# A decoder trunk that streams its weights: a weight ring by last use, and other places for the seven-product pairs of the up panels

## The chip, the core and the metric

The kernel runs on one core of one Trainium2 chip. The metric is the time of one execution on the device in microseconds (us), the median of several runs. The engines of the core that matter here: PE (TensorE, matrix multiplications), DVE (VectorE, operations of two tensors), ACT (ScalarE, scaled copies and functions), POOL (GpSimd, which here issues transfers) and SP (SyncE, whose queue issues the transfers of weights). Each engine works through its own list of instructions in order, and waits for the others by semaphores.

## What is computed

Two decoder layers on 256 tokens of 2048 channels, in float32. A layer adds the output of a mixer (gated linear attention in layer 0, forgetting attention in layer 1, each with heads that attend to 256 memory tokens) and then that of a channel mixer, which has most of the work:

```python
def conv_ffn(h, w_up, conv_w, conv_b, w_down):
    u = causal_dwconv(h @ w_up, conv_w, conv_b)
    a, val = split_cols(u, [FFN_HIDDEN, FFN_HIDDEN])
    return (jax.nn.silu(a) * val) @ w_down
...
    for i in range(DEPTH):
...
        h = rmsnorm(x, norm_ffn[i])
        x = x + conv_ffn(h, ffn_w_up[i], ffn_conv_w[i], ffn_conv_b[i], ffn_w_down[i])
    return rmsnorm(x, norm_final)
```

`FFN_HIDDEN` is 5632, so `w_up` has 2048 x 11264 numbers and `w_down` 5632 x 2048, and all weights together are read once from the chip's memory in an execution.

## The kernel before

**Units.** The weights lie in memory as a list of units of 128 x 1024 float32 numbers (512 KB). For each unit `split_unit` issues one transfer on SP into a raw slot (L232), ACT rounds it to the matmul's type (`whi`, L242), and DVE takes the rest, `wlo` = raw - `whi` (L243). There are five buffers of each. PE multiplies activations that are split in the same way, in three terms (high by high, low by high, high by low), so a single unit is twelve matmuls into four accumulators (L421), eight that read `whi` and four that read `wlo`.

**The ring of raw slots.** `raw_slot` hands out raw slots by a running index, modulo the length of the list `slots`. The list has five slots of its own tile, `home`, in the whole program. In the channel mixer two `guest` slots (tile `raw2`) are appended at the start and cut off at the end; since the modulus changes from 5 to 7 and back, the next index after such a change can fall on any slot. The guest tile comes from a pool in which the mixer's last blocks (`blk`) lie before it: they are transposed by DVE (L1637) and stored by SP to memory (`far<-blk`, L659), to be read back in another layout (L664).

**Panels and pairs.** The up projection goes in 11 panels of 16 units, the down projections in panels between groups of them (after the up panels 0 to 4, 5 to 7 and 8 to 10). In some places two neighbouring units are done as a "pair with sevens", in `pair_steps`: a scheme of seven products p1 to p7 in place of eight, 21 matmuls instead of 24. It needs four casts on ACT (L391, named w1 to w4 here by their order), four subtractions for their low parts on DVE (L392) and four subtractions of raw blocks on DVE (L446 to L449), one built on the other; w3 is cast from the second's result, w4 from the last's. A panel with one pair has it in place 6 of the 16 (counted from 0). The up panels in `MORE_IN` have two pairs, of the units 6 and 7 and 11 and 12, in places 4 and 9. The pairs' token sums are ready from the start of the channel mixer or of the first panel.

**After a panel's last pair** `early` puts together the results of its products: L1513 and L1514 on ACT, then on DVE L1515, which adds p6, and L1516 to L1518, then L1520 on ACT. At the panel's end `late` scales and adds the four accumulators (L1524) and transposes them (L1475); POOL stores the result and loads it back in runs of tokens.

**Taps.** Of each panel so turned, ACT makes the three taps of the convolution (L1425, 12 of 128 x 256 each for a half panel), DVE adds them (L1432, twice), ACT takes the silu (L1438), DVE multiplies by the gate (L1445) and splits the product (L537 on ACT, L538 on DVE) for the down projection; some products also get token sums (L485 to L488, L696, L697). `tick`, called after each unit and twice after a pair, hands out these steps by a credit per unit, so they stand between the units' casts and subtractions.

**Order.** The program is written in this order; `high_priority` moves loads, casts and subtractions of the units ahead of PE's use, and `issue_after` keeps a step behind a named instruction. The order of each engine's list is fixed when the kernel is built.

Of the kernel before, what the change touches and what calls it, by code (L numbers as in the profile page):

```python
# [37 lines left out]
MORE_IN = (1, 2, 5, 6, 7, 8, 9, 10)  # L38
SCRATCH = 4096
RAWS = 5  # L40


LEVELS = (64, 16, 4)
# [2 lines left out]
NUNIT = 1024  # L46
# [102 lines left out]
def _trunk(ctx: ExitStack, tc: tile.TileContext, xt, xtok, memt, wp, wgu, gns, gfin, cnv, par, msk, out):  # L149
    nc = tc.nc  # L150
    where, _ = _layout()
# [34 lines left out]

    loads, casts, lows, ends, last_mm, sent = [], [], [], [], [], []
    home = rear.tile([P, RAWS * NUNIT], F32, name="raw")
    slots, taken = [home[:, i * NUNIT : (i + 1) * NUNIT] for i in range(RAWS)], [0]

    def raw_slot():

        taken[0] += 1
        return slots[taken[0] % len(slots)]
    scratch = [sm]
    parked = []

# [194 lines left out]
            lows.append(V.tensor_tensor(lo[:, :n], src, hi[:, :n].bitcast(F32), ALU.subtract))  # L392
        return hi, lo

    def pair_steps(units, src, sums, flip, pool, early, late, ahead=0):

        bank = {}
        fast, slow = ("p1", "p5", "p7", "p6"), ("p2", "p3", "p4", "x")
        accs, works = (slow, fast) if flip else (fast, slow)
        tags = {n: ("acc", 4) for n in accs}  # L400
        tags.update(zip(works, (("o", 1), ("s", 2), ("s", 2), ("t", 1))))
        begun = set()
        sums = dict(sums)
        n = len(units)
        single = [k for k in range(n) if k not in sums and k - 1 not in sums]
        plan = []
        at = 0
        while at < n:
            if at + ahead in sums:
                plan.append(at + ahead)  # L410
                at += 2
            else:
                plan.append(single.pop(0))
                at += 1
        end = [k for k in plan if k in sums]

        def mm(name, x, w, last):
            if name not in bank:
                tag, bufs = tags[name]
                bank[name] = (pacc.tile([P, 512], F32, name="acc", tag="acc") if tag == "acc" else work(tag, bufs))  # L420
            r = TE.matmul(bank[name], x, w, start=name not in begun, stop=last)  # L421
            begun.add(name)
            return r

        def tok(k, b):
            return [src[k][:, part, b * P : (b + 1) * P] for part in range(2)]

        def three(name, x, w, last=False):
            for i, (a, b) in enumerate(((0, 0), (1, 0), (0, 1))):
                r = mm(name, x[a], w[b], last and i == 2)  # L430
            return r

        places = (("p2", 0, 0), ("p4", 1, 0), ("p3", 0, 1), ("x", 1, 1))
        for k in plan:
            if k in sums:
                with tc.high_priority(offset=AHEAD):
                    ra, rb = raw_slot(), raw_slot()
                    with tc.issue_after(loads[-1].ins):
                        for t, (off, _, w) in ((ra, units[k]), (rb, units[k + 1])):
                            loads.append(nc.sync.dma_start(t, wp[off : off + P * w].rearrange("(p n) -> p n", p=P)))  # L440
                st = [[sums[k][:, part, j, :] for part in range(2)] for j in (3, 0, 1, 2)]
                done = k == end[-1]
                w1 = split_more(ra[:, :512], 512)
                w2 = split_more(rb, 1024)
                with tc.high_priority(offset=AHEAD):
                    V.tensor_tensor(ra[:, :512], ra[:, 512:], ra[:, :512], ALU.subtract)  # L446
                    V.tensor_tensor(ra[:, 512:], rb[:, 512:], ra[:, 512:], ALU.subtract)  # L447
                    V.tensor_tensor(rb[:, 512:], rb[:, 512:], ra[:, :512], ALU.subtract)
                    summed = V.tensor_tensor(rb[:, :512], rb[:, :512], rb[:, 512:], ALU.subtract)  # L449
                three("p1", tok(k, 0), [t[:, :512] for t in w1], done)  # L450
                three("p2", tok(k + 1, 0), [t[:, :512] for t in w2])
                three("p3", st[3], [t[:, 512:] for t in w2])
                with tc.issue_after(summed.ins):
                    w3 = split_more(ra, 1024)
                three("p5", st[0], [t[:, :512] for t in w3], done)
                three("p7", st[2], [t[:, 512:] for t in w3], done)
                w4 = split_more(rb, 1024)
                three("p6", st[1], [t[:, 512:] for t in w4], done)
                last_mm.append(three("p4", tok(k + 1, 1), [t[:, :512] for t in w4]))
                if done:  # L460
                    with tc.issue_after(casts[-1].ins), tc.issue_after(lows[-1].ins):
                        early(bank)
                yield -1
                yield -1
                continue
            else:
                w = split_unit(units[k])
                last = k == n - 1
                steps = [(low, *place) for low in range(2) for place in places]
                if last:  # L470
                    steps.sort(key=lambda t: places.index(t[1:]))
                for low, name, b, h in steps:
                    for part in range(2 - low):
                        r = mm(name, tok(k, b)[part], w[low][:, h * 512 : (h + 1) * 512], last and low == 1)
                    if last and low:
                        ends.append(r)
                        late(b, h, bank[name])
                last_mm.append(r)
            yield k
# [875 lines left out]
    def down_pair(l, p, f, src, sums, flip, pool, temps, then=None):  # L1355

        def early(bank):
            t0, t1 = temps()
            S.activation(t0, bank["p1"], AF.Copy)
            add_to(f)(0, t0)  # L1360
            V.tensor_tensor(t0, bank["p6"], t0, ALU.add)
            V.tensor_tensor(t1, bank["p7"], t0, ALU.add)
            add_to(f)(1, t1)
            add_to(f + 1)(1, t1)
            add_to(f + 1)(1, bank["p5"])
            V.tensor_tensor(t0, bank["p5"], t0, ALU.add)
            add_to(f + 1)(0, t0)

        def late(b, h, a):
            held_back = then is not None and h and not b and then.rooms is not None  # L1370
            with tc.issue_after(then.turned[-1].ins) if held_back else nullcontext():
                add_to(f + h)(b, a)
            if then is not None:
                then(f + h, b)

        return pair_steps(where["down", l, p, f], src, sums, flip, pool, early, late)

    def add_out(key, src, then=None, spare=None, last=None, first=0, hooks=None, late=1):

# [23 lines left out]
    def ffn(l, nx, h, m, ys, zs, landing, then, pool, temps, last=None, spare=None):  # L1403
        with tc.tile_pool(name=f"ffn{l}", bufs=1) as fp:
# [3 lines left out]
            up_sums = {k: held("usum", k) for k in (*SEVEN_UP, SEVEN_MORE)}  # L1408
            rooms = {i: held("dsum", i) for i in range(2)}
            guest = pool.tile([P, 2 * NUNIT], F32, name="raw2")  # L1410
            slots.extend(guest[:, i * NUNIT : (i + 1) * NUNIT] for i in range(2))
            cw = fp.tile([P, 4 * 88], F32, name="cw")
            nc.sync.dma_start(cw, cnv[l])
            taps = [fp.tile([P, 2, 2, T + i], F32, name=f"tap{i}") for i in range(3)]
# [2 lines left out]
            count = [0, 0, 0]  # L1417
            sums = {}
# [85 lines left out]
            def up_pair(j):  # L1504

                count[2] += 1
                second = j // 4 in MORE_IN
                turns = [turn(j + 2 * h_, 7 if not h_ and j // 4 + 1 in MORE_IN else 8) for h_ in range(2)]
                u = {}

                def early(bank):
                    u.update({(b, h_): temps(2 * b + h_) for b in range(2) for h_ in range(2)})
                    S.activation(u[0, 1], bank["p1"], AF.Copy)  # L1513
                    S.activation(u[0, 0], bank["p1"], AF.Copy, scale=scale(0))  # L1514
                    V.tensor_tensor(u[0, 1], bank["p6"], u[0, 1], ALU.add)  # L1515
                    V.tensor_tensor(u[1, 0], bank["p7"], u[0, 1], ALU.add)  # L1516
                    V.tensor_tensor(u[0, 1], bank["p5"], u[0, 1], ALU.add)
                    V.tensor_tensor(u[1, 1], bank["p5"], u[1, 0], ALU.add)  # L1518
                    for b, h_ in ((0, 1), (1, 0), (1, 1)):
                        S.activation(u[b, h_], u[b, h_], AF.Copy, scale=scale(b))  # L1520

                def late(b, h_, a):
                    with tc.issue_after(turned_last[0].ins) if h_ and not b else nullcontext():
                        V.scalar_tensor_tensor(u[b, h_], a, scale(b), u[b, h_], ALU.mult, ALU.add)  # L1524
                    turns[h_](b, u[b, h_])

                return pair_steps(where["up", l, j], h, {k: up_sums[k] for k in (*SEVEN_UP, SEVEN_MORE)[: 1 + second]},
                                  count[2] % 2, pool, early, late, 2 * second)

            def first(k):  # L1530
                {2: lambda: nx.land(landing[0]), 3: nx.take, 8: nx.col,
# [64 lines left out]
            else:  # L1596
                hooks = {(2, 3): then.land, (2, 5): then.land, (2, 7): then.take, (3, 1): then.take, (3, 2): then.land,
                         (3, 5): then.take}
                for f, step, at in ((2, f2, 3), (3, f3, 0)):
                    for u in range(at, 8):  # L1600
                        step(u)
                        hooks.get((f, u), int)()
            del slots[RAWS:]

    def preparing(name, dst, pool, far, kept=None, tag="blk", queue=nc.sync):

# [204 lines left out]
```

## Time and profile before

| what | value |
|---|---|
| median of three runs | 2221.41 us (2220.82 to 2221.58) |
| profiled execution | 2219.84 us |
| its span in the profile | 2218.0 us |
| mean granted clock of TensorE | 0.997 |
| HBM read, written | 469.62 MB, 43.79 MB |
| transfers of units on SP (`raw<-wp`, 512 KB) | 741, 4.6 us from issue to landing |

In a row of a timeline stand the start (us from the span's start), the time until the end of the last of the instructions grouped in it, engine, line, operation, output and inputs by the program's names, shapes, and the count; in brackets how long the engine was idle ahead of it, and what released it. `SPq` is SP's queue of transfers. Matmuls overlap by a part of their length, so their rate is read from start to start. PE's clock (PEclk) is 1 at full rate.

### The profile page before, as it was taken

The page shows a single profiled execution, that of the slowest core. Times are in us where ns is not written, and L with a number is a line of the kernel's source. Part 1 is how long each engine was busy: PE and PEld are TensorE (multiplying, and loading weights), DVE is VectorE, ACT ScalarE, POOL GpSimd, SP SyncE. Part 2 cuts the span into 40 slices and gives each one's busy share as a digit, 9 for nine tenths or more (in the row PEclk, how much of TensorE's full clock was granted, in tenths as well). Part 3 has the DMA queues.
Part 4 walks back from the last instruction along what each step waited for, and adds up shares of the span by engine and source line. Part 5 has one row for each costly group of instructions (what it writes and reads, how often), then busy time and mean ns, then how long its engine had stood idle before and what let it go on. Part 6 is the DMA issues. An engine that isn't in the chain of part 4 may idle for free.

```text
span 2218.0 us, 30190 instructions
## 1 busy us (share of the span) xinstructions
PE 2196.9 (99%) x10285; PEld 1846.7 (83%) x10285; DVE 1828.6 (82%) x2715; ACT 1437.8 (65%) x2280; POOL 136.8 (6%) x257
## 2 busy tenths in 40 slices
PE   9999999999999999999999999999999999999998
PEld 7888888878888888888888998877888888888886
DVE  7768976679988889889987569668998888988996
ACT  6655655557887568647865555445788657765874
POOL 0000000001100000001010000000100000100000
PEclk9999999999999999999999999999999999999999
DMA  9766666776777667666877667666687667776683
GB/s 360 260 222 217 199 207 230 252 231 223 258 250 239 199 228 256 231 207 224 268 246 245 219 207 235 224 217 223 224 263 248 222 203 245 242 236 211 230 283 113
DMA packets 166291, 515.41 MB, mean 232 GB/s; under 512 B 20780, under 2 KB 42552, under 8 KB 166136
## 3 DMA queue, kind: packets, MB, share of 16 engines
q1 hardware_dynamic: 149064, 460.99, 63.2%
q0 software_dynamic: 16496, 51.71, 7.4%
q8 instruction: 80, 1.31, 0.2%
q10 hardware_dynamic: 576, 0.79, 0.1%
q14 instruction: 75, 0.61, 0.1%
HBM read 469.62 MB, written 43.79 MB: 231 GB/s over the span
## 4 chain that ended last, share of the span: by engine, by line
PE 96%; DVE 2%; ACT 1%; DMA 1%; issue 0%; SPq 0%; DVEq 0%; ACTq 0%
PE acc L421 29%; PE acc L347 26%; PE ps_s L421 15%; PE ps_o L421 7%; PE ps_t L421 7%; PE acc L273 3%; PE acc L318 3%; PE ps_s L347 2%; PE acc L377 2%; PE acc L271 1%; PE ps_s L1044 0%; DMA raw<-wp 0%; ACT whi L242 0%; PE ps_o L710 0%; PE ps_s L710 0%
## 5 line engine op out<-in xcount | busy, mean ns | idle before, releaser
L243 DVE TENSOR_TENSOR wlo<-raw,whi 128x1024 fp32r<-128x1024 f32 (+2 forms) x685 | 812.5, 1200 | 222.9 <-ACT whi L242 200.8
L242 ACT ACTIVATE whi<-raw 128x1024 fp32r<-128x1024 f32 (+2 forms) x685 | 704.3, 1045 | 347.8 <-PE acc L347 131.2
L347 PE MATMUL acc<-whi,B 128*128 128x512 f32 (+3 forms) x1248 | 290.9, 369 | 0.0
L391 ACT ACTIVATE whi<-raw 128x1024 fp32r<-128x1024 f32 (+1 forms) x184 | 173.7, 953 | 179.4 <-DVE raw L447 65.7
L347 PEld LDWEIGHTS acc<-whi,B 128*128 128x128 f32 x1248 | 226.8, 188 | 28.1
L392 DVE TENSOR_TENSOR wlo<-raw,whi 128x1024 fp32r<-128x1024 f32 (+1 forms) x184 | 198.3, 1084 | 26.8 <-ACT whi L391 23.8
L421 PE MATMUL acc<-whi,mix 128*128 128x512 f32 x746 | 191.7, 392 | 8.7 <-ACT whi L242 8.7
L421 PE MATMUL acc<-whi,B 128*128 128x512 f32 x720 | 186.9, 389 | 0.0
L421 PEld LDWEIGHTS acc<-whi,mix 128*128 128x128 f32 x746 | 141.2, 189 | 38.7 <-ACT whi L242 9.2
L347 PE MATMUL acc<-wlo,B 128*128 128x512 f32 (+3 forms) x624 | 159.1, 369 | 0.0
L421 PEld LDWEIGHTS acc<-whi,B 128*128 128x128 f32 x720 | 135.1, 188 | 28.5 <-ACT whi L242 0.5
L347 PEld LDWEIGHTS acc<-wlo,B 128*128 128x128 f32 x624 | 114.2, 188 | 14.6
L1425 ACT ACTIVATE tap<-yzu,cw 128x256 f32<-128x256 f32 x264 | 120.7, 534 | 5.4 <-DMA yzu<-far 5.4
L1425 ACT ACTIVATE tap<-fvt,cw 128x256 f32<-128x256 f32 x264 | 120.2, 530 | 3.1 <-DMA fvt<-far 3.1
L1432 DVE TENSOR_TENSOR tap<-tap,tap 128x1024 f32<-128x1024 f32 x88 | 106.7, 1213 | 9.0 <-ACT tap L1425 9.0
L421 PE MATMUL acc<-wlo,mix 128*128 128x512 f32 x373 | 105.0, 392 | 0.0
L421 PE MATMUL acc<-wlo,B 128*128 128x512 f32 x360 | 103.8, 389 | 0.0
L421 PE MATMUL ps_s<-whi,mix 128*128 128x512 f32 x374 | 103.8, 389 | 0.0
L421 PE MATMUL ps_s<-whi,B 128*128 128x512 f32 x324 | 89.9, 389 | 0.0
L421 PEld LDWEIGHTS acc<-wlo,mix 128*128 128x128 f32 x373 | 70.6, 189 | 14.8
L421 PEld LDWEIGHTS ps_s<-whi,mix 128*128 128x128 f32 x374 | 70.2, 188 | 14.6
L421 PEld LDWEIGHTS acc<-wlo,B 128*128 128x128 f32 x360 | 67.6, 188 | 14.0
(503 smaller groups left out, 3912.8 us busy)
## 6 DMA issues: line engine op xcount, KB each, us to landing
raw<-wp SPq DMA_DIRECT2D x741, 512.0 KB, 4.6
fvt<-far POOLq DMA_DIRECT2D x100, 128.0 KB, 5.2
raw<-wp SPq DMA_DIRECT2D x32, 384.0 KB, 3.4
far<-yu POOLq DMA_DIRECT2D x22, 512.0 KB, 3.0
far<-yzu POOLq DMA_DIRECT2D x22, 512.0 KB, 3.0
yzu<-far POOLq DMA_DIRECT2D x88, 128.0 KB, 4.8
raw<-wp SPq DMA_DIRECT2D x24, 388.0 KB, 3.5
x<-xtok SPq DMA_DIRECT2D x8, 512.0 KB, 7.0
```

The lines of the kernel that those rows point to most:

```text
L242: casts.append(S.activation(hi[:, s], raw[:, s], AF.Copy))
L243: lows.append(V.tensor_tensor(lo[:, s], raw[:, s], hi[:, s].bitcast(F32), ALU.subtract))
L271: mm = TE.matmul(acc[p][c][:, :T], w[:, s], both[:, 0, :], start=False, stop=end and j == 3)
L273: mm = TE.matmul(acc[p][c], w[:, s], both, start=u == j == 0, stop=end and j == 3)
L318: mm = TE.matmul(acc[b][:, :n], src[kcs[j] - base][:, part, b * P : (b + 1) * P], w, start=u == 0 and low == part == j == 0, stop=u == end ...
L347: mm = TE.matmul(acc[b][:, :n], src[kc - base][:, part, b * P : (b + 1) * P], ready[low][:, j * room : j * room + n], start=i == low == pa ...
L377: mm = TE.matmul(acc[b][:, :n], src[kc - base][:, part, b * P : (b + 1) * P], w, start=i == low == part == j == 0, stop=i == end and low = ...
L391: casts.append(S.activation(hi[:, :n], src, AF.Copy))
L392: lows.append(V.tensor_tensor(lo[:, :n], src, hi[:, :n].bitcast(F32), ALU.subtract))
L421: r = TE.matmul(bank[name], x, w, start=name not in begun, stop=last)
L1425: S.activation(by_run(taps[i][:, s, c, i:]), zs[slot][:, :, 2 * c + s], AF.Copy if i else AF.Identity, bias=0.0 if i else w[3], scale=w[2 ...
L1432: V.tensor_tensor(taps[0], taps[0], taps[n][:, :, :, :T], ALU.add)
```

## The change

The list `slots` is kept in order of last use: `raw_slot` takes the first and puts it at the end. In the channel mixer the two guest slots wait in `coming` until the first pair, which puts them in front of the list and so takes them; at the end they are taken out of the list, whose order stays. `pair_steps` takes a table from place to pair in the place of a shift. With `UP_STEPS` the pairs of an up panel with two stand at places 3 and 10 instead of 4 and 9; where there is one, it stays at 6, and the down panels' pairs stay where they are.

```diff
+UP_STEPS = ({6: 6}, {3: 6, 10: 11})
...
-    slots, taken = [home[:, i * NUNIT : (i + 1) * NUNIT] for i in range(RAWS)], [0]
+    slots, coming = [home[:, i * NUNIT : (i + 1) * NUNIT] for i in range(RAWS)], []
 
     def raw_slot():
 
-        taken[0] += 1
-        return slots[taken[0] % len(slots)]
+        slots.append(slots.pop(0))
+        return slots[-1]
...
-    def pair_steps(units, src, sums, flip, pool, early, late, ahead=0):
+    def pair_steps(units, src, sums, flip, pool, early, late, at_step):
...
         while at < n:
-            if at + ahead in sums:
-                plan.append(at + ahead)
+            if at in at_step:
+                plan.append(at_step[at])
                 at += 2
...
                 with tc.high_priority(offset=AHEAD):
+                    slots[:0] = coming
+                    del coming[:]
                     ra, rb = raw_slot(), raw_slot()
...
-        return pair_steps(where["down", l, p, f], src, sums, flip, pool, early, late)
+        return pair_steps(where["down", l, p, f], src, sums, flip, pool, early, late, {k: k for k in sums})
...
-            slots.extend(guest[:, i * NUNIT : (i + 1) * NUNIT] for i in range(2))
+            guests = [guest[:, i * NUNIT : (i + 1) * NUNIT] for i in range(2)]
+            coming.extend(guests)
...
-                                  count[2] % 2, pool, early, late, 2 * second)
+                                  count[2] % 2, pool, early, late, UP_STEPS[second])
...
-            del slots[RAWS:]
+            slots[:] = [s for s in slots if not any(s is g for g in guests)]
```

Line numbers behind the change are larger by 1 (L232 is L233, L421 is L422), by 3 from `pair_steps` on (L440 is L443, L659 is L662) and by 4 or so in the up panels (L1432 is L1436, L1515 is L1519).

**Place 1: SP's queue at the entry of layer 1's channel mixer.** Before, from the store of the last but one block (`far_13328<-blk_13314`) on; `raw_130` is the home tile, `raw2` the guest tile, L440 the loads of the first pair:

```order
L659 DMA far_13328<-blk_13314 128x1024
L232 DMA raw_130<-wp 128x1024
L664 DMA yzu_13525<-far_13328 32x4x256
L232 DMA raw_130<-wp 128x1024
L664 DMA yzu_13525<-far_13328 32x4x256 x3
L232 DMA raw_130<-wp 128x1024 x2
L659 DMA far_13503<-blk_13489 128x1024
L232 DMA raw2_13538<-wp 128x1024
L440 DMA raw2_13538<-wp 128x1024 x2
L232 DMA raw_130<-wp 128x1024 x2
```

The same stretch of the changed kernel:

```order
L662 DMA far_13328<-blk_13314 128x1024
L233 DMA raw_130<-wp 128x1024 x2
L667 DMA yzu_13525<-far_13328 32x4x256 x4
L233 DMA raw_130<-wp 128x1024 x7
L662 DMA far_13503<-blk_13489 128x1024
L443 DMA raw2_13538<-wp 128x1024 x2
L667 DMA yzu_13526<-far_13503 32x4x256
L233 DMA raw_130<-wp 128x1024
```

Seven loads into the home tile stand ahead of the last store now, where two stood, and behind it come the pair's loads into the guest tile, with no single unit's load into that tile ahead of them.

**Place 2: DVE's list at the second pair of layer 0's up panel 6**, from the pair's raw subtractions to the addition of its product p6 (L1515, after L1519). `wlo` of 128x1024 from L392 are the pair's low parts, those from L243 single units'. Before:

```order
L446 TENSOR_TENSOR raw_130<-raw_130 128x512
L392 TENSOR_TENSOR wlo_7459<-raw2_4432,whi_7458 128x1024
L447 TENSOR_TENSOR raw_130<-raw2_4432,raw_130 128x512
L448 TENSOR_TENSOR raw2_4432<-raw2_4432,raw_130 128x512
L449 TENSOR_TENSOR raw2_4432<-raw2_4432 128x512
L392 TENSOR_TENSOR wlo_7476<-raw_130,whi_7475 128x1024
L392 TENSOR_TENSOR wlo_7486<-raw2_4432,whi_7485 128x1024
L243 TENSOR_TENSOR wlo_7507<-raw2_4432,whi_7506 128x1024
L1432 TENSOR_TENSOR tap0_4435<-tap0_4435,tap1_4436 128x1024
L243 TENSOR_TENSOR wlo_7526<-raw_130,whi_7525 128x1024
L1432 TENSOR_TENSOR tap0_4435<-tap0_4435,tap2_4437 128x1024
L1515 TENSOR_TENSOR fvt_4412<-ps_t_7383,fvt_4412 128x512
```

After:

```order
L1436 TENSOR_TENSOR tap0_4435<-tap0_4435,tap1_4436 128x1024
L450 TENSOR_TENSOR raw_130<-raw2_4432,raw_130 128x512
L393 TENSOR_TENSOR wlo_7480<-raw2_4432,whi_7479 128x1024
L1436 TENSOR_TENSOR tap0_4435<-tap0_4435,tap2_4437 128x1024
L451 TENSOR_TENSOR raw2_4432<-raw2_4432,raw_130 128x512
L452 TENSOR_TENSOR raw2_4432<-raw2_4432 128x512
L393 TENSOR_TENSOR wlo_7497<-raw_130,whi_7496 128x1024
L393 TENSOR_TENSOR wlo_7507<-raw2_4432,whi_7506 128x1024
L244 TENSOR_TENSOR wlo_7528<-raw2_4432,whi_7527 128x1024
L1449 TENSOR_TENSOR cv_7544<-tap0_4435 128x512
L244 TENSOR_TENSOR wlo_7558<-raw_130,whi_7557 128x1024
L1519 TENSOR_TENSOR fvt_4412<-ps_t_7366,fvt_4412 128x512
```

The two tap additions (L1432, now L1436) moved from behind the pair's subtractions to between them, and the gate's multiplication (L1445, now L1449) from behind the addition of p6 to ahead of it. From that addition to the last raw subtraction of the next panel's first pair (L449, now L452), DVE's list has seven subtractions for single units before and five after.

## The prediction

> **What bounds the kernel now.** I read the busy table first, then the waits of PE, then the timelines around each wait.
>
> ```profile
> span 2218.0 us, 30190 instructions
> PE 2196.9 (99%) x10285; PEld 1846.7 (83%) x10285; DVE 1828.6 (82%) x2715; ACT 1437.8 (65%) x2280; POOL 136.8 (6%) x257
> PE acc L421 <- ACT whi L242: 8.7, 1, 8.7
> PE ps_t L421 <- ACT whi L391: 0.9, 1, 0.9
> ```
>
> The first two rows say that PE is busy for 2196.9 of 2218.0 us. The change adds or removes no matmul, so it can win only where PE waits or runs at a low clock, and lose only where it makes PE wait. The two rows of waits (sum, count, longest, in us) are the two largest waits of the FFN matmuls: 8.7 us for a cast of a weight unit, 0.9 us for a cast of a pair. The profiled execution took 2219.84 us, 1.57 us less than the median of the runs, 2221.41; I add up against 2219.84 and put the 1.57 back at the end.
>
> **Part 1, the ring: the wait at the entry of layer 1's channel mixer.**
>
> ```profile
> 1482.39 0.85 SPq L232 DMA_DIRECT2D raw<-wp  x2
> 1495.16 0.33 SPq L659 DMA_DIRECT2D far<-blk  x1
> 1497.78 0.33 SPq L232 DMA_DIRECT2D raw<-wp  x1
> 1493.04 0.61 PE L347 MATMUL acc<-wlo,B 128*128 128x512 f32 x2
> 1501.28 1.06 ACT L242 ACTIVATE whi<-raw 128x1024 fp32r<-128x1024 f32 x1 [2.82 <-DMA raw<-wp]
> 1502.39 3.78 PE L421 MATMUL acc<-whi,mix 128*128 128x512 f32 x8 [8.73 <-ACT whi L242]
> 1502.40:1507.70 5.30, 5.30 (x13) 0.50 0.52 155
> 1507.70:1513.00 5.30, 5.30 (x25) 1.00 0.97 275
> raw<-wp SPq DMA_DIRECT2D x741, 512.0 KB, 4.6
> ```
>
> Before, the index jumps onto a guest slot for the first unit. A guest slot lies in memory that the block stored at 1495.16 still holds, so the load behind that store leaves at 1497.78, the cast runs at 1501.28 and PE starts at 1502.39. The last matmul before it started at about 1493.27 (the second of two, one rate step after 1493.04), so the next could have started at 1493.49: 8.9 us lost. Then come 13 matmuls in 5.30 us at a granted clock of 0.50 (the windows' columns are us, PE busy and count, clock, DMA share, GB/s), where the next window holds 25. At the full rate, 10.88 us for 48 matmuls or 0.2267 us each, 13 take 2.95 us: 2.35 us lost. Together 11.3 us.
>
> ```profile
> 1032.79 10.88 PE acc L421 x48
> ```
>
> After, the order on SP puts seven loads into home slots ahead of that store, and only the two loads of the first pair behind it. PE can go on at 1493.5. The pair stands behind six units, so it is needed at 1493.5 + 6 x 2.72 = 1509.8. Its loads can leave at 1497.8, and two loads at 4.6 us from issue to landing are there before 1504; the ACT casts and DVE subtractions of a pair (some 5 us by the rows of part 2) just fit, and the first product needs only the first half-cast. I take the whole 11.3 us. Bounds: 8.9 if the clock dips anyway, and about 2 less again if the pair is late.
>
> [...]
>
> **Entry of layer 0.**
>
> ```profile
> 461.23 0.33 SPq L659 DMA_DIRECT2D far<-blk  x1
> 466.35 0.90 SPq L440 DMA_DIRECT2D raw<-wp  x2
> 470.69 0.63 ACT L391 ACTIVATE whi<-raw 128x512 fp32r<-128x512 f32 x1 [0.30 <-DMA raw<-wp]
> 477.50 0.73 PE L421 MATMUL ps_t<-whi,usum 128*128 128x512 f32 x2 [0.92 <-ACT whi L391]
> ```
>
> Here the pair's loads leave at 466.35 behind a single load that also waited for the store; the chain cast, subtractions, cast ends 0.92 us late. After, the pair's loads are the first behind the store, 0.4 us or more sooner, and that single unit's cast and subtraction (1.06 and 1.13 us) are done by then. I take 0.9; bounds 0.4 and 0.9.
>
> **Part 2, the places of the pairs.** In each layer there are three places where an up panel with two pairs follows another one with tap work for the engines in between: A (panel 1 to 2), B (6 to 7), C (9 to 10). There DVE, not PE, is near its limit:
>
> ```profile
> 841.10:883.40 42.30, 42.26 (x187) 34.66 (x186) 41.88 (x53) 33.28 (x54) 5.50 (x10) 1.00 0.77 248
> 1032.60:1074.90 42.30, 42.30 (x187) 34.70 (x186) 41.94 (x54) 33.94 (x55) 5.51 (x10) 1.00 0.75 244
> ```
>
> The columns are us, busy us of PE, PE's weight loads, DVE, ACT and POOL. In panels 7 and 10 DVE is busy for 41.88 and 41.94 of 42.30 us. It has no slack, so any idle time put upon it is late work. I follow B.
>
> ```profile
> 817.87 0.69 DVE L392 TENSOR_TENSOR wlo<-raw,whi 128x512 fp32r<-128x512 f32 x1 [1.18 <-ACT whi L391]
> 822.84 0.61 PE L421 MATMUL ps_o<-whi,B 128*128 128x512 f32 x2
> 825.96 1.22 DVE L1432 TENSOR_TENSOR tap<-tap,tap 128x1024 f32<-128x1024 f32 x1
> 828.50 0.39 PE L421 MATMUL ps_t<-wlo,usum 128*128 128x512 f32 x1
> 829.37 0.68 DVE L1515 TENSOR_TENSOR fvt<-ps_t,fvt 128x512 f32<-128x512 f32 x1
> 829.97 3.48 DVE L243 TENSOR_TENSOR wlo<-raw,whi 128x1024 fp32r<-128x1024 f32 x3
> 835.11 0.68 DVE L1445 TENSOR_TENSOR cv<-tap 128x512 f32<-128x512 f32 x1
> 852.08 0.61 PE L421 MATMUL acc<-whi,B 128*128 128x512 f32 x2
> 853.33 0.68 DVE L449 TENSOR_TENSOR raw<-raw 128x512 f32<-128x512 f32 x1
> 854.11 1.06 ACT L391 ACTIVATE whi<-raw 128x1024 fp32r<-128x1024 f32 x1 [0.86 <-DVE raw L449]
> 854.12 1.83 PE L421 MATMUL acc<-whi,usum 128*128 128x512 f32 x6
> 855.79 0.63 PE L421 MATMUL ps_s<-whi,B 128*128 128x512 f32 x2
> ```
>
> PE starts panel 6's second pair at 822.84 and panel 7's first pair at 852.08, 29.24 us later: 9 single units of 2.72 and a pair of 4.76. The deadline of DVE is the pair's last subtraction, L449: it ends at 854.01, ACT casts its result at 854.11, and the six matmuls from 854.12 reach 855.79 after 1.67 instead of 1.36 us. So L449 at 1.93 us after the pair's start costs 0.31 us, and its deadline is 1.62 us after the start.
>
> How DVE gets there: L1515 adds the product p6, whose last matmul ends at 828.89, 6.05 us after the pair began. In between DVE subtracted for two units and made the two tap additions (L1432, 1.13 us apart from the next), so it came to L1515 at 829.37 with hardly a wait. From there to L449's end it works without a gap for 24.64 us.
>
> **After**, two things stand otherwise in DVE's order. The two tap additions move ahead, into the pair's own chain of subtractions, so ahead of L1515 stand only two unit subtractions and one L1445. DVE is there early and idles until p6, 6.05 us after the pair's start, whatever lead it had. Behind L1515 stand 5 unit subtractions instead of 7, and otherwise the same work: 24.64 - 2 x 1.13 = 22.4 us (three L243 take 3.40 us from 829.97). So the last subtraction ends 6.05 + 22.4 = 28.4 us after the pair began. PE has 7 units and a pair until the next pair: 7 x 2.72 + 4.76 = 23.8, deadline 23.8 + 1.62 = 25.4. **3.0 us late.** PE loses 5.4 us of cover, DVE loses only 2.3 us of work.
>
> ```profile
> 532.25 0.68 DVE L1515 TENSOR_TENSOR fvt<-acc,fvt 128x512 f32<-128x512 f32 x1
> 541.52 0.75 DVE L1524 SCALAR_TENSOR_TENSOR fvt<-ps_o,ny,fvt 128x512 f32<-128x512 f32 x1 [0.98 <-PE ps_o L421]
> 554.87 0.69 DVE L449 TENSOR_TENSOR raw<-raw 128x512 f32<-128x512 f32 x1
> 1020.81 0.68 DVE L1515 TENSOR_TENSOR fvt<-acc,fvt 128x512 f32<-128x512 f32 x1
> 1044.72 0.68 DVE L449 TENSOR_TENSOR raw<-raw 128x512 f32<-128x512 f32 x1
> 1045.55 1.07 PE L421 MATMUL ps_s<-whi,usum 128*128 128x512 f32 x4
> 1046.61 0.73 PE L421 MATMUL ps_t<-whi,usum 128*128 128x512 f32 x2
> ```
>
> A: from 532.25 to 555.56 are 23.3 us with 0.98 idle, 22.3 of work; after, as many unit subtractions but one L1445 (0.60 from 835.11) less: 21.7, so 6.05 + 21.7 - 25.4 = 2.4 us late. C: from 1020.81 to 1045.40 are 24.6; two unit subtractions and one L1445 less, one small token sum (0.2) more: 21.9, 2.6 us late. Three places make 8.0 us a layer, 16.0 us in two. The wait is a pair's own: behind it on PE stand the units whose weights are ready, so nothing is made up, but the time lost once lets DVE catch up, and the loss doesn't carry over into the next panel. Gone are the small waits at the same spots, 0.31 at B, 0.15 at C (four matmuls from 1045.55 to 1046.61, 1.06 instead of 0.91) and their like at three more: 1.1 us. Bounds for one place: 0, if DVE had slack that I do not see, and 4 (my 3.0 and a cast, 1.06, that ACT does late). I take the sum of the rows, since each is a count of instructions on an engine without gaps.
>
> At first pairs that follow a down panel or a panel with one pair there is more time or no tap work; DVE's stretch behind L1515 is at most 17 us at panels 6 and 9 by the same durations, against 19.4 needed. I cost them, the down panels and the second pairs (two more units ahead of them) at nothing; were that cover gone, each would show some tenths.
>
> **The sum.** -11.3 - 0.9 - 1.1 + 16.0 = +2.7 us: 2222.5 profiled, 2224 as a median.
>
> **Rivals.**
> 1. *DVE's wait does not bite*: the idle time before L1515 is filled, or ACT and PE take the pair's parts in an order that leaves a later deadline; each place costs 0 to 1 us. For it: PE's busy row shows that DVE hardly stops it anywhere now. Against it: panels 7 and 10 have 0.4 us of slack. Then -13.3 + 0 to 6: 2208 to 2214 as a median, about 2211. Chance 0.20.
> 2. *Slower, by the clock*: each new wait brings the half clock, as the 8.73 us did, at 2.35 us a place. It decides as soon as the idle stretch is long enough for that; 0.92 us at 477.50 was not, 8.73 was. Six times 2.35 are 14.1 us: about 2238; two places of six, 2229. Against it: the wait at a pair falls into two, for the cast behind the second subtraction and for that behind the last, of 1 to 2 us each. [...] Chance 0.10.
> 3. *The ring does not free the entry*: unit 0 waits for something else than the store (a home slot still read by layer 1's last projection), and the wait stays. Then -2.0 + 16.0: 2235. Against it: the loads at 1482.39 left 13 us ahead of the store. Chance 0.06.
>
> **How the numbers follow.** My forecast has 0.64: 2224, with its own range of 2219 to 2229 (places of 1.9 to 3.5 us). About 0.2%, 4.4 us, is what a measurement of this kernel can tell from no change. Faster by that needs less than 1.5 us a place, slower more than 2.95: of the 0.64 I put 0.42 within and 0.20 slower, 0.02 faster. With rival 1 (0.18 faster, 0.02 within), 2 and 3 (slower): faster 0.20, same 0.44, slower 0.36. The range goes from rival 1's middle, 2211, to 2233, where part of rival 2 lies.
>
> **What would show it.** Right: no wait of PE near the entry of layer 1's mixer and no half clock there; in the waits of PE some 2 to 3 us at six places behind DVE's last subtraction or the casts of a pair (A, B, C in each layer); DVE idle for about 2 us before the addition of p6, released by PE. Wrong: DVE reaching that addition without a wait; waits of less than 1.5 us at the six places; the granted clock falling behind them; a new wait of the first pair of layer 1 at its loads.

## The result

The changed kernel took 2229.2 us (median of five runs, 2227.6 to 2231.7) against 2221.4 of the kernel before: a ratio of 1.0037 with a 95% interval of 1.0023 to 1.0050, so 5 to 11 us slower. The forecast, 2224, was 5 us too low. The range, up to 2233, holds the time, but only by the part that was put there for rival 2: the forecast's own range ended at 2229. That the change would be told apart as slower had 0.36, less than the 0.44 of no difference. The profiled execution took 2228.63 us, 8.8 more than before.

The busy table of the profile after and its largest waits of PE (sum in us, count, longest):

```profile
span 2226.9 us, 30234 instructions
PE 2200.6 (99%) x10285; PEld 1846.8 (83%) x10285; DVE 1828.4 (82%) x2715; ACT 1434.6 (64%) x2280; POOL 136.9 (6%) x257
PE ps_s L422 <- ACT whi L392: 7.3, 4, 1.8
PE acc L422 <- ACT whi L392: 5.2, 4, 1.4
PE ps_t L422 <- ACT whi L392: 1.9, 4, 0.9
```

The counts of each engine are what they were; PE is busy for 3.7 us more. The wait of 8.7 us for a single unit's cast (L242, now L243) is gone, and in its place stand twelve waits of up to 1.8 us for the casts of pairs (L391, now L392).

**The entry of layer 1's channel mixer.** A window, then PE, DVE and SP's queue there, after:

```profile
1502.00:1521.00 19.00, 19.00 (x84) 15.31 (x82) 11.20 (x19) 6.61 (x15) 0.00 (x0) 1.00 0.61 192
1501.12 0.62 PE L348 MATMUL acc<-wlo,B 128*128 128x512 f32 x2
1504.31 1.19 DVE L244 TENSOR_TENSOR wlo<-raw,whi 128x1024 fp32r<-128x1024 f32 x1
1505.41 0.71 DVE L1641 STREAM_TRANSPOSE blk<-x 128x512 f32<-128x512 f32 x1
1490.08 15.78 SPq L233 DMA_DIRECT2D raw<-wp  x7
1505.53 0.33 SPq L233 DMA_DIRECT2D raw<-wp  x1
1506.15 0.33 SPq L662 DMA_DIRECT2D far<-blk  x1
1512.00 0.80 SPq L443 DMA_DIRECT2D raw<-wp  x2
1522.07 0.74 PE L422 MATMUL ps_t<-whi,usum 128*128 128x512 f32 x2 [0.92 <-ACT whi L392]
```

PE is busy for all 19 us of the window, at the full clock: the wait and its half clock, 11.3 us, are gone. What is new is the last row. The pair's loads leave at 1512.00, and two things make that late. The store is issued only at 1506.15, when DVE has transposed the block (L1641): that is 5.0 us after the mixer's last row on PE (1501.12), where it was 2.1 before (1493.04 to 1495.16), as other work of DVE now stands in between, such as the subtraction at 1504.31 for a unit loaded early. And the last of the seven loads, the one at 1505.53, left just ahead of the store and is still moving (4.4 us to landing; the sixth was issued 5 us earlier), and the store lands at 1511.98, so the pair's loads leave 5.85 us after it was issued; before, when the loads ahead of the store had landed by 1488.73, that took 2.6 us (1495.16 to 1497.78). Together they leave 6.1 us later against PE's work, and the pair's last cast comes about 1.1 us late.

**Place B.** DVE, PE and ACT between the second pair of panel 6 and the first of panel 7, after:

```profile
827.81 0.62 PE L422 MATMUL ps_o<-whi,B 128*128 128x512 f32 x2
831.28 1.22 DVE L244 TENSOR_TENSOR wlo<-raw,whi 128x1024 fp32r<-128x1024 f32 x1
833.98 0.69 DVE L1519 TENSOR_TENSOR fvt<-ps_t,fvt 128x512 f32<-128x512 f32 x1 [1.47 <-PE ps_t L422]
851.61 0.61 PE L422 MATMUL acc<-whi,B 128*128 128x512 f32 x2
853.42 0.39 PE L422 MATMUL ps_s<-wlo,usum 128*128 128x512 f32 x1
855.67 0.70 DVE L452 TENSOR_TENSOR raw<-raw 128x512 f32<-128x512 f32 x1
855.16 1.19 PE L422 MATMUL acc<-whi,usum 128*128 128x512 f32 x4 [1.35 <-ACT whi L392]
857.59 0.73 PE L422 MATMUL acc<-whi,usum 128*128 128x512 f32 x2 [1.24 <-ACT whi L392]
```

This is the chain that was forecast. The pair starts at 827.81; DVE comes to the addition of p6 early and stands idle for 1.47 us until PE has it, 6.17 us after the pair's start. The last subtraction (L452) ends at 856.37, 22.4 us later, as counted. The next pair starts 23.8 us after the one before, and PE waits twice in it: from 853.42 to 855.16 is 1.51 more than a matmul's 0.23, and from 855.16 to 857.59 is 1.52 more than the 0.91 of four, of which the cast is 1.4, as one of the four is 0.11 slower than the rest. That is 2.9 us; 3.0 were forecast. The same reading gives 2.4, 2.9 and 2.6 us at A, B and C in each layer, 15.8 in all, where 16.0 was forecast.

**What was not in the sum** is the clock behind these waits. PE's windows behind A, C and (layer 1) B:

```profile
555.40:557.70 2.30, 2.30 (x6) 1.82 (x7) 2.30 (x3) 2.30 (x3) 1.86 (x4) 0.50 0.76 214
1051.60:1053.90 2.30, 2.30 (x10) 1.91 (x11) 2.30 (x4) 2.30 (x3) 2.05 (x4) 1.00 1.08 230
1903.20:1905.50 2.30, 2.30 (x7) 1.82 (x6) 2.30 (x4) 2.30 (x4) 1.34 (x3) 0.50 0.94 232
```

At three of the six places (A of layer 0, B and C of layer 1) PE runs at a granted clock of 0.50 for 3.4 us each, with six or seven in 2.30 us where ten go in; at the other three it stays at 1.00. From the starts of the matmuls this costs 1.4 + 1.6 + 1.4 = 4.4 us. So the 8.9 us of the span add up: -11.3 at layer 1's entry, +1.1 for the late pair there, -0.9 at layer 0's entry, -1.1 for the small waits replaced, +15.8, +4.4, and 0.3 each at single units of the last down panels (the waits at 1115 and 2162 us, for casts of L242, grew from 0.45 to 0.76) make +8.6.

### The profile page after: what moved, and what is told of

The parts are those of the page before. It is cut to its first block, busy times and chain, and to the rows that moved or that the text cites. A ratio compares the mean times of both kernels' runs of the same rounds, so it can differ in the third digit from the quotient of the medians.

```text
span 2226.9 us, 30234 instructions
## 1 busy us (share of the span) xinstructions
PE 2200.6 (99%) x10285; PEld 1846.8 (83%) x10285; DVE 1828.4 (82%) x2715; ACT 1434.6 (64%) x2280; POOL 136.9 (6%) x257
## 4 chain that ended last, share of the span: by engine, by line
PE 92%; DVE 5%; DMA 1%; issue 1%; ACT 1%; SPq 0%; DVEq 0%; ACTq 0%
PE acc L348 26%; PE acc L422 26%; PE ps_s L422 14%; PE ps_o L422 7%; PE ps_t L422 7%; PE acc L274 3%; PE acc L319 3%; PE ps_s L348 2%; PE acc L378 2%; PE acc L272 1%; DMA raw<-wp 1%; DVE wlo L244 1%; DVE wlo L393 1%; DMA far<-blk 0%; ACT whi L392 0%
## 5 line engine op out<-in xcount | busy, mean ns | idle before, releaser
L243 ACT ACTIVATE whi<-raw 128x1024 fp32r<-128x1024 f32 (+2 forms) x685 | 701.7, 1045 | 321.9 <-PE acc L348 140.5
L392 ACT ACTIVATE whi<-raw 128x1024 fp32r<-128x1024 f32 (+1 forms) x184 | 173.8, 953 | 205.9 <-DVE raw L450 54.5
L422 PE MATMUL acc<-whi,mix 128*128 128x512 f32 x746 | 192.0, 390 | 0.0
L422 PE MATMUL acc<-whi,B 128*128 128x512 f32 x720 | 187.1, 390 | 0.0
L422 PEld LDWEIGHTS acc<-whi,mix 128*128 128x128 f32 x746 | 140.4, 188 | 29.4
L422 PEld LDWEIGHTS acc<-whi,B 128*128 128x128 f32 x720 | 135.6, 188 | 28.3
L1436 DVE TENSOR_TENSOR tap<-tap,tap 128x1024 f32<-128x1024 f32 x88 | 107.4, 1221 | 22.5 <-ACT tap L1429 22.3
L422 PE MATMUL acc<-wlo,mix 128*128 128x512 f32 x373 | 105.2, 389 | 0.0
L422 PE MATMUL ps_s<-whi,mix 128*128 128x512 f32 x374 | 105.1, 391 | 0.0
L422 PE MATMUL acc<-wlo,B 128*128 128x512 f32 x360 | 103.2, 389 | 0.0
L422 PE MATMUL ps_s<-whi,B 128*128 128x512 f32 x324 | 89.7, 389 | 0.0
L422 PEld LDWEIGHTS ps_s<-whi,mix 128*128 128x128 f32 x374 | 70.8, 189 | 14.8
L422 PEld LDWEIGHTS acc<-wlo,mix 128*128 128x128 f32 x373 | 70.0, 188 | 14.6
L422 PEld LDWEIGHTS acc<-wlo,B 128*128 128x128 f32 x360 | 67.6, 188 | 14.0
```

The lines of the kernel that those rows point to most:

```text
L243: casts.append(S.activation(hi[:, s], raw[:, s], AF.Copy))
L392: casts.append(S.activation(hi[:, :n], src, AF.Copy))
L1436: V.tensor_tensor(taps[0], taps[0], taps[n][:, :, :, :T], ALU.add)
```

## The experiments

Each ran beside the kernel before on the same chip (2221.3 us in the first four, 2220.8 in the last four); ratios have their 95% interval.

**1. The ring alone.**

```diff
-UP_STEPS = ({6: 6}, {3: 6, 10: 11})
+UP_STEPS = ({6: 6}, {4: 6, 9: 11})
```

> The ring by last use alone, the pairs at places 4 and 9 as before. Theory: the ring gives the gain and only the places cost. The entry of layer 1's channel mixer loses its 8.9 us of waiting and its half clock (together 11.4 us); the first pair there may still wait about 1 us for its loads; layer 0's entry gains about 1. The small waits at the second two-pair panels (0.2 to 0.3 us at A, B, C) stay. About 2221.4 - 11.5 = 2210 us (2208 to 2212). Rival: the cost comes from the ring too (guest slots handed out in another order hold up loads at the pairs); then waits of 1 us or more show up at A, B and C with the old places as well, and the time stays above 2214.

2209.8 us, ratio 0.9948 (0.9934 to 0.9961). No pair at A, B or C waits more than 0.25 us. The ring is a gain of 11.5 us, and the whole loss comes with the places.

**2. The places alone.** The five edits of the ring are undone (three are shown), `UP_STEPS` is kept.

```diff
-    slots, coming = [home[:, i * NUNIT : (i + 1) * NUNIT] for i in range(RAWS)], []
+    slots, taken = [home[:, i * NUNIT : (i + 1) * NUNIT] for i in range(RAWS)], [0]
...
-        slots.append(slots.pop(0))
-        return slots[-1]
+        taken[0] += 1
+        return slots[taken[0] % len(slots)]
...
-            guests = [guest[:, i * NUNIT : (i + 1) * NUNIT] for i in range(2)]
-            coming.extend(guests)
+            slots.extend(guest[:, i * NUNIT : (i + 1) * NUNIT] for i in range(2))
```

> The old ring by index, the pairs at places 3 and 10. Theory: the places alone cost what the changed kernel shows at six places, 15.9 us of waits and 4.3 us at half clock behind three of them, less the small waits that they replace (1.1): some 16 to 20 us, 2237 to 2242 us, with the wait of 8.7 us at the entry of layer 1 still there. At A of layer 0 fewer instructions stand behind the addition of p6 than in the changed kernel, so that one may be 1.5 us instead of 2.4. Rival: the waits need the new ring; then the time is near 2222.

2245.9 us, ratio 1.0104 (1.0091 to 1.0118): 24.6 us slower, above the 16 to 20 expected. Its waits of PE:

```profile
PE acc L422 <- ACT whi L243: 10.8, 2, 8.9
PE ps_s L422 <- ACT whi L392: 5.9, 3, 2.3
PE acc L422 <- ACT whi L392: 5.2, 4, 1.3
PE ps_t L422 <- ACT whi L392: 4.5, 4, 2.9
```

The pairs wait as in the changed kernel, and the 8.9 us are there. Three things are above the expectation. A waits 3.0 us in layer 0 and 2.9 in layer 1, not the 1.5 and 2.4 that I had counted; in layer 0 DVE comes to the addition of p6 at 537.39 without a wait, 1.9 us after the last matmul of p6 ended, so it was late there already. The first row has a second wait, of 1.9 us: the single unit behind the store at layer 0's entry, whose load left at 465.97 before and leaves at 467.02 here. The lists of all engines up to there are the same in both, so the places don't explain this, and the cause stays open. And the profiled execution took 2241.1 us, the low end of the runs (to 2247.0), so the median has some 5 us that its trace doesn't show. The mean granted clock does: 0.995 in the profiled execution and 0.992 in the other three, which is some 13 us more at half clock; at 1.4 us lost for 3.4 us of it, as above, that makes 5 to 6 us, an estimate. The two halves, -11.5 and +24.6, therefore don't add to the +7.8 of both.

**3. The tap additions two steps later** (for the first half panel; one step for the second). Same instructions, same places.

```diff
-                turns = [turn(j + 2 * h_, 7 if not h_ and j // 4 + 1 in MORE_IN else 8) for h_ in range(2)]
+                turns = [turn(j + 2 * h_, (9 if not h_ else 9) if j // 4 + 1 in MORE_IN else 8) for h_ in range(2)]
```

> The changed kernel, with the taps of a panel that is followed by a two-pair panel handed out from tick 9 on instead of 7 and 8. In DVE's list the two tap additions go from the middle of the second pair's subtractions to just ahead of the addition of p6, as before the change, and the gate's multiplication behind it. Same instructions, same 7 units between the pairs. Theory (DVE stands idle until p6 with work behind it): counted in the list, DVE's stretch from the addition of p6 to the next pair's last subtraction shrinks from 22.1 to 22.8 us to 18.0 to 19.9, against 19.4 that are there: waits of at most 0.3 us at the six places, no half clock there, 2229.2 - 20 = 2209 us (2207 to 2212). Rival (7 units and a pair are too little cover for DVE's work between the pairs, wherever the additions stand): the waits stay near 2.5 us and the time near 2229.

2211.2 us, ratio 0.9953 (0.9940 to 0.9965). DVE's rows at place B:

```profile
828.63 1.22 DVE L1436 TENSOR_TENSOR tap<-tap,tap 128x1024 f32<-128x1024 f32 x1
829.76 1.22 DVE L244 TENSOR_TENSOR wlo<-raw,whi 128x1024 fp32r<-128x1024 f32 x1
830.90 0.68 DVE L1519 TENSOR_TENSOR fvt<-ps_t,fvt 128x512 f32<-128x512 f32 x1
849.72 0.69 DVE L452 TENSOR_TENSOR raw<-raw 128x512 f32<-128x512 f32 x1
```

With the additions where they fill the time until p6, DVE reaches the addition without a wait, and L452 ends 19.5 us after it instead of 22.4. PE's waits at B and C are at most 0.1 us, at A at most 0.6; the mean granted clock of the profiled execution is 0.998, where the changed kernel has 0.996. 18.0 of the 19.4 us that the places cost (2229.2 - 2209.8) are gone, with 7 units between the pairs as in the changed kernel. Cover alone can't explain them.

**4. One step later,** for the first half panel only.

```diff
-                turns = [turn(j + 2 * h_, 7 if not h_ and j // 4 + 1 in MORE_IN else 8) for h_ in range(2)]
+                turns = [turn(j + 2 * h_, (8 if not h_ else 8) if j // 4 + 1 in MORE_IN else 8) for h_ in range(2)]
```

> The same with 8 instead of 7 for the first half panel only, a smaller dose: in the list one of the two tap additions goes ahead of p6's addition behind the pair, and the gate's multiplication behind it. Counted in the list, the stretch behind p6's addition is 19.2 us at A, 21.6 at B, 20.3 at C, against 19.4 that are there. Theory: waits of about 0 at A, 1.8 at B, 0.5 at C in each layer, 4.6 us in all where the changed kernel has 15.9, and less or no half clock: 2212 to 2215 us. Rival (cover): no change, near 2229.

2219.1 us, ratio 0.9989 (0.9980 to 0.9997): between the two, as a smaller dose should be, but 4 us above the top of what was expected. PE waits 0.3, 2.2 and 1.0 us at A, B and C of layer 0 and 1.8, 2.2 and 1.0 in layer 1, 8.7 us where the count gave 4.6. DVE's rows at B and C of layer 0 and at A of layer 1 say why:

```profile
838.66 0.75 DVE L1528 SCALAR_TENSOR_TENSOR fvt<-acc,ny,fvt 128x512 f32<-128x512 f32 x1 [0.45 <-PE acc L422]
1032.23 0.75 DVE L1528 SCALAR_TENSOR_TENSOR fvt<-ps_o,ny,fvt 128x512 f32<-128x512 f32 x1 [0.78 <-PE ps_o L422]
1574.86 0.69 DVE L1449 TENSOR_TENSOR cv<-tap 128x512 f32<-128x512 f32 x1 [0.89 <-ACT tap L1442]
1580.95 1.23 DVE L1436 TENSOR_TENSOR tap<-tap,tap 128x1024 f32<-128x1024 f32 x1 [0.53 <-ACT tap L1429]
```

The count of instructions takes DVE as never waiting behind p6. Once it is ahead it waits there for other things, for the panel's accumulators or for ACT's taps and silu, and that time is late work as well.

**5 and 6. Eight units between the pairs, in two ways.**

```diff
-UP_STEPS = ({6: 6}, {3: 6, 10: 11})
+UP_STEPS = ({6: 6}, {4: 6, 10: 11})
```

> The new ring, the pairs at places 4 and 10: 8 units from a panel's second pair to the next first one, where the changed kernel has 7 and the places of before 9. Theory (DVE's list behind the addition of p6): counted in the list that stretch is 23.2, 22.8 and 23.1 us at A, B and C, and 22.1 us are there; with 0.98 of the counted time, 0.3 to 0.7 us of wait, and some 0.4 more, as the last run was above its count: 0.7 to 1.1 us a place, 4 to 7 us in all, of which 1.5 are there with places 4 and 9 as well. 2212 to 2216 us, no half clock. Rival (cover: the loss goes with the units between the pairs): half way between 9 units (2209.8) and 7 (2229.2), 2219.5.

```diff
-UP_STEPS = ({6: 6}, {3: 6, 10: 11})
+UP_STEPS = ({6: 6}, {3: 6, 9: 11})
```

> The new ring, the pairs at places 3 and 9: also 8 units in between. Theory: by the list 21.6, 23.4 and 23.1 us at A, B and C against 22.1: nothing at A, 0.9 and 0.6 us at B and C, some 0.4 more each by the last runs: 2 to 3 us a layer, 2212 to 2214 us, with A the smallest, other than in the run with 4 and 10. Rival (cover): as that run, 2219.5, with A, B and C alike.

2213.4 us (ratio 0.9967, 0.9955 to 0.9980) and 2215.7 us (0.9979, 0.9971 to 0.9988). Neither is at 2219.5. The first lies in its expectation; the second is 1.7 us above it. With places 3 and 9 the waits are 0.3, 1.4 and 1.4 us at A, B and C of layer 0, A the smallest as counted, but 1.5, 1.4 and 1.8 in layer 1, where A was counted as nothing. In 6 DVE comes to the addition of p6 without a wait at all six places, and PE still waits there, so idle time is not all of it either: the units between the pairs, the cover, matter too. But eight units cost much less than half of what seven cost (3.6 and 5.9 us over 2209.8, against 19.4), and the two ways of having eight differ.

**7 and 8. The two ideas of the ring apart**, both with the places of before. In 7 the guests are put in front of the list when the channel mixer begins; in 8 the old index stays, and the guests join at the first pair.

```diff
-            coming.extend(guests)
+            slots[:0] = guests
```

> The ring by last use with the places of before, but the two guest slots are put in front of the list as soon as the channel mixer begins, not at its first pair. Theory: what gives the gain is that no single unit takes a guest slot while the block's store is out; here the first two units' loads stand behind that store again in both layers, and the wait at the entry of layer 1 (8.9 us) and its half clock (2.4) come back: 2209.8 + 11 = 2221 us (2219 to 2223). Rival: the order by last use itself gives the gain (the slot handed out is free sooner); then it stays near 2210.

```diff
-        slots.append(slots.pop(0))
-        return slots[-1]
+        taken[0] += 1
+        return slots[taken[0] % len(slots)]
...
-                    slots[:0] = coming
+                    slots.extend(coming)
```

> The other half: the old running index, but the guests join the list only at the first pair; the places of before. Theory: the same loads stand ahead of the store as in the new ring, so the gain is all here: 2210 us (2208 to 2212), with at most some tenths where the index falls on a slot in use. Rival: as above, the order by last use gives it; then the wait at the entry stays and the time is near 2221.

8 took 2209.1 us (0.9949, 0.9937 to 0.9962), as fast as the ring by last use. 7 took 2230.7 us (1.0045, 1.0032 to 1.0057). PE and SP in 7 at the entries of layers 0 and 1:

```profile
458.16 0.34 SPq L662 DMA_DIRECT2D far<-blk  x1
460.82 0.81 SPq L233 DMA_DIRECT2D raw<-wp  x2
465.75 1.65 PE L422 MATMUL acc<-whi,B 128*128 128x512 f32 x3 [9.09 <-ACT whi L243]
1512.43 2.93 PE L422 MATMUL acc<-whi,mix 128*128 128x512 f32 x6 [8.81 <-ACT whi L243]
```

The wait is back, in layer 0 as well. The expectation had named both layers and priced only one; with the second wait of 9.1 us and its half clock (0.50 from 465.75 to 469.50) the time is accounted for. So what gains 11.5 us is that the guests join late; the order by last use gains nothing that these runs can tell.

## Why the prediction was near, and what it missed

- **The ring, -11.3 and -0.9 us**: right (experiments 1 and 8). The new wait of 1.1 us at layer 1's first pair stood only in the bounds ("about 2 less again if the pair is late"). The step that failed is the time at which the pair's loads can leave, 1497.8, and with it the 1504 for their landing. It took over both the issue of the store, which came 2.9 us later against PE's work as DVE had other work ahead of the transposition, and its 2.6 us with nothing moving ahead of it, which became 5.85 behind a load just issued. The trace of before had a store of that kind, at layer 0's entry: 461.23, with the next loads from 465.97 on.
- **The places, +16.0 us**: right in mechanism, place and size, 15.8 in the profile. The idle time until p6 is seen, and experiment 3 fills it and takes the loss away. The list of an engine without slack, with the durations of the trace, gave each wait within 0.1 us.
- **Covers costed at nothing**: nearly right; 0.6 us at two single units of the last down panels. These two waits are 0.75 to 0.81 us in every run with a second pair at place 10, and 0.41 to 0.46 in every run with it at 9.
- **The mis-sized term is the clock.** It stood as rival 2 at 0.10, with 14.1 us for six places and "two places of six, 2229" beside it; the forecast itself had it at zero, with the reason that a wait in two pieces of 1 to 2 us would keep the clock. No row of before shows that: it has 0.92 us with the clock kept and 8.73 us with 0.50 behind it, so the zero was an estimate. At three places of six the clock fell: 4.4 us, most of what the forecast lacks. So what came is the forecast and half of rival 2 together, which the chances treated as one or the other. Each of the three stretches lasted 3.41 us; the longest wait of such a place was 1.98 us from start to start, and the half clock came at half of them (the last section has the rows). Between the sum, 2222.5 for a profiled execution, and the 2228.6 that it took lie 6.1 us: these 4.4, the 1.1 of the late pair and the 0.6 at the down panels. The 4.4 are this execution's: the mean clock, 0.996 in it, is 0.998 in two of the other four (2227.6 and 2230.8 us), which by the lengths in the traces (3.41 us a stretch, and 3.8 us at the end of the kernel before, 6.5 of the changed one) leaves room for two half-clock stretches at most (an estimate), so the spread of the runs isn't the clock's alone.
- **Its own signs**: of those for being right, the waits at six places and DVE's idle time released by PE came (1.2 to 2.3 us). Of those for being wrong two came as well: the clock falling behind the waits, and the late first pair of layer 1.
- **Rival 1** (DVE's wait does not bite) and **rival 3** (the ring doesn't free the entry) fell, by the rows after and by experiment 1.

The ring with the places of before, or the late guests alone, is faster than both kernels: 2209.8 and 2209.1 us.

## What to carry to other kernels

- Work moved to where an engine would only have got ahead leaves a hole where it used to fill a wait. On an engine that is busy for 41.9 of 42.3 us, count its list from the point at which it must wait for another engine to its next deadline: that predicted each wait of the changed kernel to 0.1 us. Add the waits inside that stretch, which a count does not see; in experiments 4 and 6 it was up to 1.8 us short.
- A new wait of PE can bring a stretch at half clock: here three of six places with waits of up to 1.98 us had one behind them, at 1.4 to 1.6 us each. Price it as a chance, not as nothing or everything.
- When slots of a ring share memory with something that is still being stored, it is the moment at which they join that counts, not the order in which slots are handed out.
- Measure the two halves of a change apart: here -11.5 us was hidden under the cost of the other half.

## What the hardware showed that was not expected

The half clock doesn't follow from the length of one wait here. At A of layer 0 and C of layer 0 PE waits in the same way in the changed kernel:

```profile
553.87 1.47 PE L422 MATMUL ps_s<-whi,usum 128*128 128x512 f32 x4 [1.82 <-ACT whi L392]
555.34 1.22 PE L422 MATMUL ps_t<-whi,usum 128*128 128x512 f32 x2
1049.88 1.20 PE L422 MATMUL ps_s<-whi,usum 128*128 128x512 f32 x4 [1.82 <-ACT whi L392]
1051.52 0.73 PE L422 MATMUL ps_t<-whi,usum 128*128 128x512 f32 x2 [0.44 <-ACT whi L392]
```

Both wait 1.82 us. Behind the first the four matmuls take 1.47 us and the next two 1.22, and the window shown above has a clock of 0.50; behind the second they take 1.20 and 0.73, with a wait of 0.44 between them, and the clock stays at 1.00.

What differs in the trace is how the wait lies against the times at which the clock changes. In the changed kernel the granted clock goes to 0.50 at 554.61, 1902.87 and 2097.43, for 3.41 us each time (and once more, at 2220.31, when PE's work has ended), and these starts are 395 and 57 times 3.413 us apart. In the kernel before it goes to 0.50 at 1497.47 and back to 1.00 at 1507.71, three times 3.413 us later; PE worked again from 1502.39, so 5.3 us of work had passed by then. In stretches of 3.41 us that are counted from 554.61, the two places look like this (us, then PE's busy us; the clock is the third column from the end):

```profile
551.20:554.61 3.41, 1.59 (x7) 1.03 (x6) 3.34 (x6) 1.44 (x2) 2.22 (x5) 1.00 0.46 187
554.61:558.02 3.41, 3.40 (x8) 2.17 (x8) 3.34 (x4) 3.41 (x4) 2.72 (x6) 0.50 0.71 199
1046.13:1049.54 3.41, 1.94 (x9) 1.28 (x7) 3.41 (x9) 0.77 (x1) 1.13 (x3) 1.00 0.38 155
1049.54:1052.95 3.41, 2.62 (x10) 1.89 (x11) 3.41 (x7) 2.84 (x4) 2.73 (x6) 1.00 0.91 286
```

At A the whole wait lies in one stretch: PE is idle for 1.82 of 3.41 us, and the next stretch has half the clock. At C the waiting falls into two, 1.47 and 0.79 us, and the clock stays. Counted in this way (in the trace of before from 1497.47) and from 6 us of the span on, the two traces have six stretches at full clock with one at 0.50 behind them. PE was idle in them for 1.82, 1.96, 1.81 and, at the kernel's end, 2.30 us after, and for all 3.41 us twice before (at layer 1's entry and at the end). In the other stretches at full clock it was idle for at most 1.47 us after and 1.64 us before. These are counts of two traces: no run moved a wait against these times with all else the same, and what sets them was not shown.
